# Delta-rule layer of a trunk kernel: what follows from a strip stands later in TensorE's order, the decays after the second keys, an own place for the substitution's tile

## Chip, cores and metric

The kernel runs on one core of a Trainium2 chip. The time is the device time of one execution in microseconds (us), shown as the median of several executions; lower is better. Inputs, weights and output are float32.

## What is computed

The reference is a trunk of four pre-norm residual layers over 256 tokens of width 1024: a pooling mixer, a gated delta-rule mixer, a latent attention, and a pooling mixer again. The change lies in the second, the delta-rule layer. Cut to what matters there:

```python
def gdn_mixer(h, w_in, conv_w, a_log, dt_bias, norm_g, w_out):
    proj = h @ w_in                               # 1024 -> 6160 columns
    qkv, gate, b_raw, a_raw = jnp.split(proj, ...)
    qkv = jax.nn.silu(causal_depthwise_conv(qkv, conv_w))
    q, k, v = jnp.split(qkv, [GDN_QK, 2 * GDN_QK], axis=-1)
    q = l2norm(...q) * (GDN_DK ** -0.5)           # 8 heads x 128
    k = l2norm(...k)                              # 8 heads x 128
    beta = sigmoid(b_raw); g = -exp(a_log) * softplus(a_raw + dt_bias)
    o = chunk_gated_delta_rule(q, k, v, g, beta)  # v: 8 heads x 256
    o = rmsnorm(o, norm_g) * silu(gate)
    return o @ w_out

def chunk_gated_delta_rule(q, k, v, g, beta):
    decay = jnp.exp(jnp.where(causal, diff, -jnp.inf))     # diff of summed g
    L = jnp.where(strict, (k_beta @ k.T) * decay, 0.0)
    sol = triangular_solve(I + L, [v_beta, k_beta * exp(g)])
    attn = jnp.where(causal, (q @ k.T) * decay, 0.0)
    ...
    # then from chunk to chunk: v_new = u - w @ state; o = q_dec @ state + attn @ v_new
```

## The kernel before

**Strips.** Every projection is cut into strips of 512 output columns over eight slices of the 1024 inputs. SyncE (SP) loads the weights in pieces of two slices, 512 KB each, into three buffers called `raw` (line 115). For float32 accuracy a slice is split in two parts: ScalarE (ACT) rounds it into `whi` (line 128), VectorE (DVE) or, for the slices named in `pool`, GpSimd (POOL) subtracts to get `wlo` (line 130). Each part has a ring of nine buffers, so that the splitting can be about a strip ahead of TensorE (PE). PE then does three products for every slice and column group. A strip that lands channel by channel (`chan=True`: keys, queries, values) is four units (pieces of weights) with 24 matmuls of 128x256 each, 96 in all; a strip of the gate is four units of 12 matmuls with 512 columns.

**The strips of the delta-rule layer**, in order: gate 0, keys 0, keys 1, queries 0, gate 1, values 0, queries 1, gate 2, values 1, values 2, values 3, gate 3, and then the output projection. After a strip of keys or queries (`channels`) ACT copies the four channel groups out of PSUM with the last tap of the convolution (`cv`, line 658), DVE adds three more taps to each (12 instructions, line 661), and ACT takes the Silu into the tile `kqT` (line 694). Values go the same way in two tiles `vc` (Silu in line 810).

**Side work.** What follows from a strip stands between the units of later strips; the lists handed to `keys`, `queries`, `gate` and `values` name it, one list for each gap after a unit (the first list after unit 0).
- `key_norms` and `query_norms` (through `squares`): PE transposes the four groups of `kqT` (8 transposes, `tp<-ident,kqT`, line 100), ACT squares them (line 705), DVE sums. `query_norms` has, on POOL, the product of `Eb` and the queries (`Gb<-Gb,kqT`, line 789) and a power for the norm.
- `lower` and `scored` (through `against`): 8 small matmuls (`aux<-kqT`), and 8 instructions on DVE that scale them by the decays `DT` into `LT` or the scores.
- `substitution`: eight DMAs write the diagonal blocks of `LT` to `d_l` in device memory (line 748), one reads them back as `Lb` (line 751), POOL does 31 pairs of instructions on `Lb`, `Tb` and `pr` (lines 756 and 760), and nine DMAs bring the result through `d_t` (line 762) into `T` (line 766). All these DMAs stand in SP's queue among the loads of weights.
- `values_turned`: 8 transposes of `vc` for two heads (`tp<-ident,vc`), and scaled copies into `vR` on ACT (line 823).
- `inverses` with `pairs`, `joined`, `turned`, `whole`, `last` (blocks of the inverse out of `T`), `news`, and the `step`s of the recurrence.
- `decays`: five Exp on ACT (line 651) over `DT` (two tiles), `Eb` (a name for the second `Gb` tile) and `eG`. Exp and Silu use different tables, and ACT loads a table when the function changes (ACT_TABLE_LOAD).

**What sets the order.** From `pinned["on"] = True` on, PE's instructions stand in the order of the program text. The other engines' order is made by a scheduler, which `later(...)` can hold back until a given instruction has been issued. Each engine works its queue strictly in order. Tiles called `big` share a pool of equal places; who gets the place of which earlier tile follows from the order of allocation, and a new owner waits for the last use by the old one. In this kernel `kqT_3639`, the output of queries 1, is given the place of `Lb`.

Of the kernel before, what the change touches and what calls it, by code (L numbers as in the profile page):

```python
# [12 lines left out]
AF = mybir.ActivationFunctionType  # L13
# [3 lines left out]
P = 128  # L17
D = 1024
S = 256
NT = S // P  # L20
# [22 lines left out]
def trunk(ctx: ExitStack, tc: tile.TileContext, x, positions, norm_g, pool_w_in, pool_w_grp,  # L43
# [3 lines left out]
    nc = tc.nc  # L47
# [22 lines left out]
    def big(name, *dims, dt=F32):  # L70
        return s4.tile([P, *dims], dt, tag="s4", name=name)
# [13 lines left out]
    def later(*instructions):  # L85

        order = ExitStack()
        for ins in instructions:
            order.enter_context(tc.issue_after(ins))
        return order  # L90


    pinned = {"on": False}
# [10 lines left out]
    mark = {}  # L104
# [333 lines left out]
    def pool_layer(i, j, hT):  # L438
# [64 lines left out]
        for g in order:  # L503
            gs = gate(g)
            if not place:
                with later(*[m for k, m in mark.items() if k != "rest"]):
                    turn_params()
                    window_counts()
            elif setups:
                with later(*[m for k, m in mark.items() if k != "rest"]):  # L510
                    setups.pop(0)()
            pT = pooled(g)
            if waiting:
                mixed(*waiting)
            waiting = (g, pT, gs)
# [46 lines left out]
    def gdn_layer(i, j, hT):  # L562
        H = GDN_H
        M = NT * H
# [13 lines left out]
        def gate(vi, *between):  # L578
            banks = project(cols_of(w_in, 2 * GDN_QK + GDN_V + vi * CW), units(KD), hT,
                            pool=() if vi else (0, 4), between=between)  # L580
            gs.append(big("gsg", NT, CW))
            for t in range(NT):
                gated = nc.scalar.activation(gs[vi][:, t, :], banks[t], AF.Silu)
            mark["gate"] = gated.ins
# [61 lines left out]
        Eb = Gb[1]  # L646

        def decays():
            with later(mark["gate"]):
                for a in (*DT, Eb, eG):  # L650
                    nc.scalar.activation(a, G if a is eG else a, AF.Exp)

# [11 lines left out]


        Q, B = 4, 32
        Tb = big("Tb", B, B)[:M * Q]
        nc.gpsimd.memset(Tb, 0.0)
        nc.gpsimd.memset(Tb.rearrange("m r c -> m (r c)")[:, ::B + 1], 1.0)
        T = [big("T", H, P) for _ in range(NT)]  # L670
# [13 lines left out]
        def channels(dst, c0, hf, which, between):  # L684

            banks = project(cols_of(w_in, c0 + hf * CW), units(KD), hT, chan=True,
                            pool=() if which else (0, 2, 4, 6), between=between)
            dst.append(big("kqT", 4, S))
            for b in range(2):
                cv = [worka("cv", S) for _ in range(2)]  # L690
                conv(*[(banks[b][:, c * S:(c + 1) * S], (c0 + hf * CW) // P + 2 * b + c, cv[c])
                       for c in range(2)])
                for c in range(2):
                    nc.scalar.activation(dst[hf][:, 2 * b + c, :], cv[c], AF.Silu)

        def squares(src, hf, which):

# [27 lines left out]
        def keys(hf, *between):  # L725
            channels(kT, GDN_QK, hf, 0, between)
# [11 lines left out]
        def lower(hf):  # L738
            for t in range(NT):
                against(LT, kT, s2, hf, t)  # L740

        def substitution():

            d_l = dram.tile([M * Q, B * B], F32, name="d_l")
            lv = d_l.rearrange("(t m d) (r c) -> t d r m c", t=NT, d=Q, r=B)
            for t in range(NT):
                for d in range(Q):
                    nc.sync.dma_start(out=lv[t, d],
                                      in_=LT[t][d * B:(d + 1) * B, :, d * B:(d + 1) * B])
            Lb = big("Lb", B, B)[:M * Q]  # L750
            nc.sync.dma_start(out=Lb, in_=d_l.rearrange("m (r c) -> m r c", r=B))
            pr = small("pr", 256, bufs=1)[:M * Q]
            for r in range(B - 1):
                n, c = B - 1 - r, r + 1
# [22 lines left out]
        def queries(hf, *between):  # L777
            channels(qT, 0, hf, 1, between)
# [52 lines left out]
        def inverses():  # L831
# [3 lines left out]


            U.extend(big("U", H, P) for _ in range(NT))
            X1 = [big("X1", H, P) for _ in range(NT)]
            for t in range(NT):
                nc.gpsimd.memset(X1[t][:, :, 32:64], 0.0)  # L840
                nc.vector.transpose(U[t].rearrange("p m c -> p (m c)"),
# [130 lines left out]
        def step(n):  # L972
            for m, stage in enumerate(stages):
                if 0 <= n - m < H:
                    stage(n - m)

        def do(f, *args):
            return lambda: f(*args)


        inv = lambda name, t: lambda: Us[name](t)
        keys(0)
        decays()
        pinned["on"] = True
        keys(1, (), (), [do(key_norms, 0)])
        queries(0, [do(lower, 0)], [do(key_norms, 1)], [do(lower, 1), substitution])
        gate(1, (), [do(query_norms, 0)], [do(scored, 0)])
        values(0)
        queries(1, (), (), [do(values_turned, 0)])
        gate(2, (), [do(query_norms, 1)], [do(scored, 1)])  # L990
        values(1)
        values(2, (), [do(values_turned, 1), inverses], [inv("pairs", 0)], [inv("pairs", 1)])
        values(3, [inv("joined", 0)], [inv("joined", 1), inv("turned", 0)],
               [do(values_turned, 2), inv("whole", 0), inv("turned", 1)],
               [inv("last", 0), inv("whole", 1)])
        gate(3, [inv("last", 1), do(news, 0)], [do(step, 0), do(values_turned, 3)],
             [do(news, 1), do(step, 1)], [do(step, 2)])
        for n in range(3, 6):
            step(n)
        return layer_out(gdn_w_out[j], yT, units(POOL_W // P), i,  # L1000
# [320 lines left out]
```

## Time and profile before

| what | value |
|---|---|
| time, median of 3 executions | 887.39 us (884.95 to 888.65) |
| the profiled execution's own time | 886.94 us |
| its span on the core | 885.2 us |
| mean granted TensorE clock | 0.975 |
| busy share of PE, DVE, ACT, POOL | 95%, 67%, 56%, 16% |
| PE's share of the chain that ended last | 83% |
| POOL's share of the same chain | 6% |
| weights and other data read from memory | 137.79 MB |

The page says how long each engine was busy in the span, then shows the span in 40 slices of 22.1 us with a digit for the busy tenths of each; a line PEclk gives the clock that TensorE was granted in each slice. Further views of the same execution list each instruction with its start, its duration and, in brackets, how long its engine stood idle before it and which instruction's end released it; and they sum such waits by line. The delta-rule layer's strips from keys 0 to the end of values 2 run from about 199 to 343 us of the span.

### The profile page before, as it was taken

Reading aid. Unit: us, or ns where it says so; the run is one execution under the profiler, and the core shown is the slowest. Engines: PE = TensorE matmul, PEld = TensorE weight load, DVE = VectorE, ACT = ScalarE, POOL = GpSimd, SP = SyncE. Lnnn points to the kernel's source line nnn. Section 1 sums busy time; section 2 is a strip of 40 time slices with the busy share of each in tenths; the row PEclk is TensorE's granted clock in tenths of the full one; section 3 lists DMA queues with packets and bytes.
Section 4 is the critical chain, followed back from the end, with each engine's and each line's share of the span. In section 5 each row is a group of like instructions: output and inputs, shape, how many; then the busy total and the mean of one; then the engine's idle time right before and its main releaser. Section 6 shows DMA issues by size and latency. Waiting matters only on the chain.

```text
span 885.2 us, 16118 instructions
## 1 busy us (share of the span) xinstructions
PE 844.9 (95%) x5967; PEld 784.7 (89%) x5967; DVE 594.7 (67%) x1144; ACT 494.6 (56%) x1009; POOL 144.1 (16%) x286
## 2 busy tenths in 40 slices
PE   7999999996899697999999999999999999999996
PEld 6999998986879597978898998999988989999986
DVE  5688776457777466646666666867877666867762
ACT  6655655467555353555556564556655565565542
POOL 4010001342249700012220201100000120000012
PEclk8999999998799799999999999999999999999999
DMA  6666556556346353222356766663444446665551
GB/s 236 200 190 202 180 176 214 156 175 184 96 119 183 88 170 105 93 78 96 123 148 195 221 169 162 187 190 97 129 143 134 146 129 204 201 202 183 191 200 49
DMA packets 111288, 140.43 MB, mean 159 GB/s; under 512 B 23340, under 2 KB 53224, under 8 KB 111208
## 3 DMA queue, kind: packets, MB, share of 16 engines
q1 hardware_dynamic: 109056, 138.17, 51.4%
q0 software_dynamic: 320, 1.06, 0.4%
q8 instruction: 47, 0.77, 0.4%
q10 hardware_dynamic: 1832, 0.16, 0.2%
q14 instruction: 33, 0.27, 0.1%
HBM read 137.79 MB, written 1.58 MB: 157 GB/s over the span
## 4 chain that ended last, share of the span: by engine, by line
PE 83%; POOL 6%; DVE 4%; DMA 2%; ACT 2%; issue 2%; SPq 0%; POOLq 0%; ACTq 0%; DVEq 0%
PE acc L96 68%; PE aux L96 12%; PE tp L100 3%; POOL Tb L760 2%; POOL pr L756 2%; DVE wlo L130 1%; DVE h L329 1%; DMA raw<-in_gdn_w_in_dram 1%; DMA gain<-in_norm_g_dram 1%; DMA Lb<-d_l 1%; DVE cv L661 1%; ACT junk L235 0%; ACT whi L128 0%; POOL xr L322 0%; DVE x L379 0%
## 5 line engine op out<-in xcount | busy, mean ns | idle before, releaser
L130 DVE TENSOR_TENSOR wlo<-raw,whi 128x512 fp32r<-128x512 f32 (+1 forms) x497 | 342.3, 710 | 190.2 <-ACT whi L128 181.7
L128 ACT CAST whi<-raw 128x512 fp32r<-128x512 f32 (+1 forms) x508 | 301.3, 617 | 269.9 <-PE acc L96 198.0
L96 PE MATMUL acc<-hTh,whi 128*128 128x256 f32 x832 | 237.5, 286 | 0.0
L96 PE MATMUL acc<-hTl,whi 128*128 128x256 f32 x832 | 236.8, 285 | 0.0
L96 PE MATMUL acc<-hTh,wlo 128*128 128x256 f32 x832 | 236.0, 284 | 0.0
L96 PEld LDWEIGHTS acc<-hTh,whi 128*128 128x128 f32 x832 | 159.5, 192 | 0.8
L96 PEld LDWEIGHTS acc<-hTl,whi 128*128 128x128 f32 x832 | 159.5, 192 | 0.4
L96 PEld LDWEIGHTS acc<-hTh,wlo 128*128 128x128 f32 x832 | 159.4, 192 | 0.1
L96 PE MATMUL acc<-whi,yTh 128*128 128x256 f32 (+1 forms) x384 | 116.8, 322 | 0.0
L96 PE MATMUL acc<-wlo,yTh 128*128 128x256 f32 (+1 forms) x384 | 116.4, 318 | 0.0
L96 PE MATMUL acc<-whi,yTl 128*128 128x256 f32 (+1 forms) x384 | 91.7, 318 | 0.0
L96 PEld LDWEIGHTS acc<-wlo,yTh 128*128 128x128 f32 x384 | 72.1, 188 | 5.0
L96 PEld LDWEIGHTS acc<-whi,yTh 128*128 128x128 f32 x384 | 71.9, 188 | 5.1
L96 PEld LDWEIGHTS acc<-whi,yTl 128*128 128x128 f32 x384 | 63.2, 188 | 5.9
L96 PE MATMUL acc<-whi,hTh 128*128 128x512 f32 (+1 forms) x144 | 58.6, 413 | 0.7 <-ACT hTh L221 0.7
L96 PE MATMUL acc<-wlo,hTh 128*128 128x512 f32 (+1 forms) x144 | 58.1, 407 | 0.5 <-DVE wlo L130 0.2
L317 POOL TENSOR_TENSOR hg<-x,gain 128x256 f32<-128x256 f32 x18 | 15.1, 843 | 260.3 <-DVE x L379 256.9
L96 PE MATMUL acc<-whi,hTl 128*128 128x512 f32 (+1 forms) x144 | 46.5, 397 | 0.0
L96 PEld LDWEIGHTS acc<-wlo,hTh 128*128 128x128 f32 x144 | 28.6, 199 | 7.1 <-DVE wlo L130 1.8
L96 PEld LDWEIGHTS acc<-whi,hTh 128*128 128x128 f32 x144 | 28.6, 199 | 7.0 <-ACT hTh L221 1.7
L96 PEld LDWEIGHTS acc<-whi,hTl 128*128 128x128 f32 x144 | 27.6, 195 | 5.9 <-DVE hTl L226 0.2
L461 POOL COPY win<-u 128x4 f32<-128x4 f32 x8 | 2.8, 353 | 177.4 <-ACT u L455 177.4
(330 smaller groups left out, 1420.2 us busy)
## 6 DMA issues: line engine op xcount, KB each, us to landing
raw<-in_pool_w_in_dram SPq DMA_DIRECT2D x60, 512.0 KB, 4.2
raw<-in_gdn_w_in_dram SPq DMA_DIRECT2D x48, 512.0 KB, 4.1
raw<-in_pool_w_out_dram SPq DMA_DIRECT2D x32, 512.0 KB, 3.7
raw<-in_mla_w_in_dram SPq DMA_DIRECT2D x24, 512.0 KB, 4.3
raw<-in_mla_w_uq_dram SPq DMA_DIRECT2D x36, 256.0 KB, 3.4
raw<-in_pool_w_grp_dram SPq DMA_DIRECT2D x16, 512.0 KB, 4.2
raw<-in_gdn_w_out_dram SPq DMA_DIRECT2D x16, 512.0 KB, 3.6
raw<-in_mla_w_ukv_dram SPq DMA_DIRECT2D x32, 256.0 KB, 3.0
```

The lines of the kernel that those rows point to most:

```text
L96: ins = nc.tensor.matmul(*args, **opts)
L100: ins = nc.tensor.transpose(*args)
L128: a = nc.scalar.copy(hi, v)
L130: b = e.tensor_tensor(out=lo, in0=v, in1=hi.bitcast(F32), op=ALU.subtract)
L317: nc.gpsimd.tensor_tensor(out=self.early[t, a], in0=xs[t][:, sl], in1=self.g[:, sl], op=ALU.mult)
L329: nc.vector.scalar_tensor_tensor(out=h[:, cut:], in0=xs[t][:, sl], scalar=r[:, 0:1], in1=self.g[:, sl], op0=ALU.mult, op1=ALU.mult)
L461: nc.gpsimd.tensor_copy(nxt[:, :, :d], cur[:, :, :d])
L661: nc.vector.scalar_tensor_tensor(out=o[:, d:], in0=ps[:, :S - d], scalar=tp(3 - d, c), in1=o[:, d:], op0=ALU.mult, op1=ALU.add)
L756: nc.gpsimd.tensor_tensor(out=pv, op=ALU.mult, in0=Lb[:, r, r + 1:, None].to_broadcast([M * Q, n, c]), in1=Tb[:, r:r + 1, :c].to_broadcast ...
L760: nc.gpsimd.tensor_tensor(out=tv, in0=tv, in1=pv, op=ALU.subtract)
```

## The change

The side work that follows from a strip of keys, queries or values stands later in PE's order, behind or near the end of the next strip: by one unit (norms of keys 0, turned values 0 and 1), two (norms of keys 1) or three units (norms of the queries). The norms of keys 0 come after the last unit of keys 1 (before: after its third unit, with `between` lists that begin with the first gap); those of keys 1, the second `lower` and the substitution after the last unit of queries 0; the norms of queries 0 and their scores in values 0; the turned values 0 after queries 1; the norms and scores of queries 1 in values 1; the turned values 1 and the inverses' first step in the third gap of values 2. The steps on the inverses follow in values 3 and gate 3, and `step(2)` and `news(1)` come after gate 3's last unit. A list that stands in the fourth place runs after the strip's last unit.

`decays` is called after keys 1 and held until the last Silu of keys 1 has been issued (`mark["kq"]`). The slices 0 and 4 of queries 0 get their subtraction on POOL. `Lb` and `Tb` keep names for their whole tiles, and the two tiles `X1` of the inverses use that memory after the substitution, so the pool gives `Lb` a place that no other tile takes.

```diff
-                with later(*[m for k, m in mark.items() if k != "rest"]):
+                with later(*[m for k, m in mark.items() if k not in ("rest", "kq")]):
...
         def decays():
-            with later(mark["gate"]):
+            with later(mark["gate"], mark["kq"]):
                 for a in (*DT, Eb, eG):
                     nc.scalar.activation(a, G if a is eG else a, AF.Exp)
...
-        Tb = big("Tb", B, B)[:M * Q]
+        Tb_ = big("Tb", B, B)
+        Tb = Tb_[:M * Q]
...
-                            pool=() if which else (0, 2, 4, 6), between=between)
+                            pool=(0, 4) if which and hf == 0 else () if which else (0, 2, 4, 6), between=between)
...
-                    nc.scalar.activation(dst[hf][:, 2 * b + c, :], cv[c], AF.Silu)
+                    mark["kq"] = nc.scalar.activation(dst[hf][:, 2 * b + c, :], cv[c],
+                                                      AF.Silu).ins
...
+        free = []
...
-            Lb = big("Lb", B, B)[:M * Q]
+            Lb_ = big("Lb", B, B)
+            Lb = Lb_[:M * Q]
+            free.extend((Lb_, Tb_))
...
-            X1 = [big("X1", H, P) for _ in range(NT)]
+            X1 = [a.rearrange("p (h a) c -> p h (a c)", h=H) for a in free]
...
         keys(0)
+        pinned["on"] = True
+        keys(1, (), (), (), [do(key_norms, 0)])
         decays()
-        pinned["on"] = True
-        keys(1, (), (), [do(key_norms, 0)])
-        queries(0, [do(lower, 0)], [do(key_norms, 1)], [do(lower, 1), substitution])
-        gate(1, (), [do(query_norms, 0)], [do(scored, 0)])
-        values(0)
-        queries(1, (), (), [do(values_turned, 0)])
-        gate(2, (), [do(query_norms, 1)], [do(scored, 1)])
-        values(1)
-        values(2, (), [do(values_turned, 1), inverses], [inv("pairs", 0)], [inv("pairs", 1)])
-        values(3, [inv("joined", 0)], [inv("joined", 1), inv("turned", 0)],
-               [do(values_turned, 2), inv("whole", 0), inv("turned", 1)],
-               [inv("last", 0), inv("whole", 1)])
-        gate(3, [inv("last", 1), do(news, 0)], [do(step, 0), do(values_turned, 3)],
-             [do(news, 1), do(step, 1)], [do(step, 2)])
+        queries(0, [do(lower, 0)], (), (), [do(key_norms, 1), do(lower, 1), substitution])
+        gate(1)
+        values(0, [do(query_norms, 0)], [do(scored, 0)])
+        queries(1, (), (), (), [do(values_turned, 0)])
+        gate(2)
+        values(1, [do(query_norms, 1)], [do(scored, 1)])
+        values(2, (), (), [do(values_turned, 1), inverses], [inv("pairs", 0)])
+        values(3, [inv("pairs", 1)], [inv("joined", 0)], [inv("joined", 1), inv("turned", 0)],
+               [inv("whole", 0), inv("turned", 1), do(values_turned, 2)])
+        gate(3, [inv("last", 0), inv("whole", 1)], [inv("last", 1), do(news, 0)], [do(step, 0)],
+             [do(step, 1), do(values_turned, 3)])
+        step(2)
+        news(1)
         for n in range(3, 6):
             step(n)
```

In the order of PE's instructions, the place where the norms of keys 0 (`kqT_2671`) are taken stands before ahead of the last unit of keys 1 (whose banks are `acc_2700` and `acc_2701`; the weights of its fourth unit begin with `whi_2829`):

```order
L96 MATMUL acc_2701<-hTh1_2267,whi_2777 128x256
L96 MATMUL acc_2701<-hTl1_2268,whi_2777 128x256
L96 MATMUL acc_2701<-hTh1_2267,wlo_2776 128x256
L100 MATMUL tp_2804<-ident_101,kqT_2671 128x128 x4
L100 MATMUL tp_2813<-ident_101,kqT_2671 128x128 x4
L96 MATMUL acc_2700<-hTh1_2267,whi_2829 128x256
L96 MATMUL acc_2700<-hTl1_2268,whi_2829 128x256
```

and now at the end of keys 1, ahead of the first matmuls of queries 0 (bank `acc_2885`):

```order
L96 MATMUL acc_2697<-hTh1_2267,whi_2807 128x256
L96 MATMUL acc_2697<-hTl1_2268,whi_2807 128x256
L96 MATMUL acc_2697<-hTh1_2267,wlo_2806 128x256
L100 MATMUL tp_2834<-ident_101,kqT_2671 128x128 x4
L100 MATMUL tp_2843<-ident_101,kqT_2671 128x128 x4
L96 MATMUL acc_2885<-hTh0_2258,whi_2890 128x256
L96 MATMUL acc_2885<-hTl0_2259,whi_2890 128x256
```

The two groups of transposes moved behind the last unit of keys 1, 24 matmuls. The number of PE's instructions is the same in both kernels.

In ACT's order, around the last Silus of keys 0 (`kqT_2671`) before:

```order
L694 ACT_TABLE_LOAD
L694 ACTIVATE kqT_2671<-cv_2672 128x256
L694 ACTIVATE kqT_2671<-cv_2673 128x256
L694 ACTIVATE kqT_2671<-cv_2684 128x256
L705 ACTIVATE sq_2809<-tp_2804 128x512
L651 ACT_TABLE_LOAD
L651 ACTIVATE DT_2496<-DT_2496 128x1024
L694 ACT_TABLE_LOAD
L694 ACTIVATE kqT_2671<-cv_2685 128x256
L705 ACTIVATE sq_2818<-tp_2813 128x512
L651 ACT_TABLE_LOAD
L651 ACTIVATE DT_2497<-DT_2497 128x1024
```

and now behind the last Silu of keys 1 (`kqT_2856`):

```order
L695 ACTIVATE kqT_2856<-cv_2858 128x256
L707 ACTIVATE sq_3046<-tp_3041 128x512
L695 ACTIVATE kqT_2856<-cv_2870 128x256
L651 ACT_TABLE_LOAD
L651 ACTIVATE DT_2496<-DT_2496 128x1024
L651 ACTIVATE DT_2497<-DT_2497 128x1024
L651 ACTIVATE Gb_2493<-Gb_2493 128x1024
L651 ACTIVATE eG_2484<-G_2483 128x16
L707 ACTIVATE sq_3055<-tp_3050 128x512
```

The Exps of `DT` left the Silus of keys 0 and stand in one block; the norms' second square (`sq_3055`) stands behind that block. Further down ACT's queue, ten casts `whi` (the last of them, `whi_3525`, out of `raw_3522`) now stand between the `cv` copies of queries 0 and its four Silus; before, two.

In SP's queue, where the substitution goes out and comes in (`raw` are weights; `d_l` and `Lb` the substitution's input), before:

```order
L115 DMA raw_3364<-in_gdn_w_in_dram 128x2x512
L748 DMA d_l_3047<-LT_2531 32x8x32 x4
L748 DMA d_l_3047<-LT_2532 32x8x32 x4
L115 DMA raw_3398<-in_gdn_w_in_dram 128x2x512
L751 DMA Lb_3056<-d_l_3047 64x1024
L115 DMA raw_3432<-in_gdn_w_in_dram 128x2x512
```

and now:

```order
L115 DMA raw_3488<-in_gdn_w_in_dram 128x2x512
L752 DMA d_l_3081<-LT_2531 32x8x32 x4
L115 DMA raw_3522<-in_gdn_w_in_dram 128x2x512
L752 DMA d_l_3081<-LT_2532 32x8x32 x2
L115 DMA raw_3556<-in_gdn_w_in_dram 128x2x512
L752 DMA d_l_3081<-LT_2532 32x8x32 x2
L115 DMA raw_3590<-in_gdn_w_in_dram 128x2x512
L757 DMA Lb_3090<-d_l_3081 64x1024
```

The eight writes of `d_l` stand three loads of weights later, with two loads among them: `raw_3522`, the second load of queries 1, now stands behind the first four writes, which need the whole first tile of `LT`. The result's way back stands now as follows, with three loads of values 3 (`raw_4189`, `raw_4233`, `raw_4287`) behind the write of `d_t` and among the reads of `T`:

```order
L115 DMA raw_4145<-in_gdn_w_in_dram 128x2x512
L768 DMA d_t_3155<-Tb_2514 64x1024
L115 DMA raw_4189<-in_gdn_w_in_dram 128x2x512
L772 DMA T_2517<-d_t_3155 32x8x32 x4
L772 DMA T_2518<-d_t_3155 32x8x32
L115 DMA raw_4233<-in_gdn_w_in_dram 128x2x512
L772 DMA T_2518<-d_t_3155 32x8x32 x3
L115 DMA raw_4287<-in_gdn_w_in_dram 128x2x512
```

Between the read of `Lb` and the write of `d_t` stand thirteen loads of weights, before twelve.

More of the change, by code (lines that the diff above doesn't have):

```diff
@@ L509, in pool_layer @@
             elif setups:
-                with later(*[m for k, m in mark.items() if k != "rest"]):
+                with later(*[m for k, m in mark.items() if k not in ("rest", "kq")]):
                     setups.pop(0)()
```

## The prediction

> **What bounds the kernel now.** First I read the page's share of TensorE (PE) and its clock in the 40 slices of 22.1 us:
>
> ```profile
> PE   7999999996899697999999999999999999999996
> PEclk8999999998799799999999999999999999999999
> ```
>
> PE is full nearly everywhere. Slices 10 to 16 (from 199 us on) are the exception, four of them with 6, 8, 6 and 7 tenths, and there the clock falls too. This is the delta-rule layer, the only place where the change moves much; at the start of the program it moves one transfer past another, which I cost at nothing. PE does the same instructions in both kernels. So the question is how much of PE's idle time goes, and how much of its slow time. Next the waits of PE in that stretch (195 to 345 us): total us, number of times, longest:
>
> ```profile
> PE tp L100 <- ACT kqT L694: 19.7, 9, 6.2
> PE tp L100 <- ACT vc L810: 6.7, 3, 3.6
> ```
>
> All 26.4 us are waits of a strip's own transposes for its Silu. One by one they are these rows of PE's timeline (start, duration, and in brackets the idle time before, with its releaser):
>
> ```profile
> 207.80 0.28 PE L96 MATMUL acc<-hTh,whi 128*128 128x256 f32 x1
> 209.81 0.28 PE L96 MATMUL acc<-hTh,wlo 128*128 128x256 f32 x1
> 213.05 1.30 PE L100 MATMUL tp<-ident,kqT 128*128 128x128 f32 x6 [2.96 <-ACT kqT L694]
> 218.68 0.69 PE L100 MATMUL tp<-ident,kqT 128*128 128x128 f32 x2 [4.33 <-ACT kqT L694]
> 252.66 0.66 PE L100 MATMUL tp<-ident,kqT 128*128 128x128 f32 x4 [1.09 <-ACT kqT L694]
> 254.36 0.46 PE L100 MATMUL tp<-ident,kqT 128*128 128x128 f32 x2 [1.04 <-ACT kqT L694]
> ```
>
> The first two rows are 17 matmuls apart, so one takes 0.118 us at full clock, a unit of 24 takes 2.8 us, a strip 11.3. Then keys 0 stop PE for 7.3 us, queries 0 for 2.1. Keys 1 stop it at 233.8 and 235.3; by the total of 19.7, keys 1 and queries 1 share the other 10.3. The waits for values are
>
> ```profile
> 332.83 0.66 PE L100 MATMUL tp<-ident,vc 128*128 128x128 f32 x4 [1.22 <-ACT vc L810]
> 337.07 1.12 PE L100 MATMUL tp<-ident,vc 128*128 128x128 f32 x4 [3.58 <-ACT vc L810]
> ```
>
> 4.8 us for values 1, which leaves 1.9 of the 6.7 for values 0. The long wait of queries 1 has another cause than its own strip. The view of the tile `Lb`, which shared its place with that output, says so:
>
> ```profile
> L756 POOL TENSOR_TENSOR pr<-Lb,Tb x31: 230/506/1056, 253.9 to 300.6; 64x31 f32<-64x31 f32 x2, 64x60 f32<-64x60 f32 x2, 64x87 f32<-64x87 f32 x2, 64x112 f32<-64x112 f32 x2
>   ACT kqT L694: 7.6, 1
> ```
>
> The first Silu of queries 1 waited 7.6 us for the last use of `Lb`, on GpSimd (POOL) up to 301 us, and PE behind it for 6.2 (the longest wait above).
>
> Second, the slow clock. The windows view, columns: us, busy us (and instructions) of PE, PEld, DVE, ACT, POOL, granted clock, DMA share, GB/s:
>
> ```profile
> 199.50:343.40 143.90, 117.44 (x793) 108.40 (x794) 96.56 (x208) 76.39 (x139) 58.56 (x87) 0.88 0.47 134
> 213.68:223.92 10.24, 5.91 (x29) 5.51 (x28) 7.67 (x24) 9.07 (x11) 1.95 (x2) 0.50 0.33 110
> 234.16:240.99 6.83, 6.15 (x30) 5.76 (x29) 3.68 (x11) 2.17 (x5) 2.84 (x3) 0.50 0.29 79
> 254.64:258.05 3.41, 3.41 (x11) 2.63 (x10) 0.69 (x1) 0.60 (x1) 2.86 (x9) 0.50 0.36 138
> 299.02:309.26 10.24, 6.38 (x18) 4.71 (x19) 3.06 (x5) 3.57 (x8) 5.11 (x11) 0.50 0.48 107
> 336.56:339.97 3.41, 2.90 (x14) 2.91 (x15) 0.00 (x0) 1.29 (x3) 0.00 (x0) 0.50 0.00 0
> ```
>
> Each stretch of half clock follows a wait of PE and lasts 3.41 us or a multiple. PE's busy time in the five, 5.91 + 6.15 + 3.41 + 6.38 + 2.90 = 24.75, would be half at full clock: 12.4 us lost. So the layer holds **26.4 + 12.4 = 38.8 us** that better order could return at most.
>
> **The change, part by part.** I followed each engine's new order with the durations of the old trace. The sum stands against the profiled execution's own 886.94 us (span 885.2 and 1.7 around it); the median of the runs is 887.39, which is 0.05% off, so one number serves both.
>
> *Norms of keys 0* move one unit, 2.8 us, later. What gated them is on ACT (first the start, then the duration):
>
> ```profile
> 211.28 1.28 ACT L694 ACT_TABLE_LOAD   x1
> 212.58 1.03 ACT L694 ACTIVATE kqT<-cv 128x256 f32<-128x256 f32 x3
> 214.50 1.28 ACT L651 ACT_TABLE_LOAD   x1
> 216.91 1.28 ACT L694 ACT_TABLE_LOAD   x1
> 218.21 0.42 ACT L694 ACTIVATE kqT<-cv 128x256 f32<-128x256 f32 x1
> ```
>
> The fourth Silu came 4.6 us behind the third, since an Exp and two table loads stood between. Without them four Silus end at about 214.0, and PE arrives at 209.9 + 2.8 = 212.8 and needs the second pair 0.5 us later. Left: about 0.5 us (between 0 and 1.2), no half clock. Before: 7.3 + 5.91/2 = 10.2. The Exps now stand behind the last Silu of keys 1, where the first `lower` needs `DT`, 24 matmuls (2.8 us) into queries 0; two table loads and three Exps are some 5 us, hidden for PE, since nothing of PE waits for `LT` until a PSUM bank is asked for again in gate 1.
>
> *Norms of keys 1* move two units, 5.7 us, later. But DVE gets there late. Its queue holds both decay tiles and the subtractions ahead of the twelve taps of keys 1:
>
> ```profile
> 213.61 2.19 DVE L643 SCALAR_TENSOR_TENSOR DT<-Gb,G,maskT 128x128 f32<-128x128 f32 x8 [1.90 <-DMA Gb<-d_g]
> 217.31 2.19 DVE L643 SCALAR_TENSOR_TENSOR DT<-Gb,G,maskT 128x128 f32<-128x128 f32 x8
> ```
>
> Before, PE stood for 7.3 us in that time and DVE caught up; now it doesn't get that pause. By my walk PE arrives at 226.7 and waits 2.3 us in two parts (bounds: 0, and twice that if two subtractions stand otherwise). Half clock follows for one stretch: 3.41/2 = 1.7. Left 4.0; before 2.5 + 6.15/2 = 5.6.
>
> *Norms of queries 0* move three units, and this is the part where I see a new wait. The casts for queries 1 now stand between the `cv` copies and the Silus of queries 0 on ACT. The last of them needs `raw_3522`, which stands on SP behind four writes of `d_l`; these wait for the second half of `LT`, which stands on DVE behind subtractions for values 0. In before the writes went at
>
> ```profile
> 243.59 3.79 SPq L748 DMA_DIRECT2D d_l<-LT  x8
> 301.14 0.46 SPq L762 DMA_DIRECT2D d_t<-Tb  x1
> 304.15 3.19 SPq L766 DMA_DIRECT2D T<-d_t  x6
> raw<-in_gdn_w_in_dram SPq DMA_DIRECT2D x48, 512.0 KB, 4.1
> ```
>
> and in the new order I get about 244.2 for the first, so four writes (1.9 us) and a load (4.1 us to landing) bring `raw_3522` at 250.2, the cast, a table load of 1.28 and the four Silus at 253.6. PE arrives at 246.2. **A wait of 6.4 us**, and half clock for one or two stretches (PE is busy in about 4.2 us of them): 2.1. Left 8.5; before 2.1 + 3.41/2 = 3.8. The bounds of the wait: nothing if the half of `LT` is done 6 us earlier, and 9 if the buffer comes free later too.
>
> *Turned values 0* move one unit: 2.8 us cover the 1.9. Left 0.
>
> *Norms of queries 1*: with an own place for `Lb` the Silus wait for DVE alone, and three units cover that. Before 7.8 + 6.38/2 = 11.0; left 0. What is late next is the substitution itself.
>
> *Turned values 1*: in before 4.8 + 2.90/2 = 6.3. The substitution starts later, I get 256.6 for 253.9, and POOL has more between its steps: the second queries' product and power fall into it as well as the first's:
>
> ```profile
> L789 POOL TENSOR_TENSOR Gb<-Gb,kqT 128x512 f32<-128x512 f32 x2 | 2.6, 1276 | 3.6 <-ACT kqT L694 3.6
> L682 POOL TENSOR_TENSOR rq<-rq,halves 128x8 f32<-128x8 f32 x2 | 3.3, 1650 | 0.1
> ```
>
> 47.2 us (253.9 to 301.1) and 2.9 more make 50, so it ends near 306.6. Then on SP: the write of `d_t`, 3.0 until the first read of `T` (301.14 to 304.15), eight reads at 0.53 and two loads among them at 0.4, so the last load, `raw_4287`, is issued near 315 and lands near 319. Its casts stand on ACT ahead of the Silu of values 1. So PE is through the turned values 1 near 321, with some 5.8 us of waits on the way, and 1.7 for a half clock. Left 7.5. Before, PE stood at this point of its work at 341.6.
>
> *The end of the layer*: `step(2)` and `news(1)` have no matmuls of gate 3 beside them now. I take 0, between 0 and 2.
>
> Sum: left 0.5 + 4.0 + 8.5 + 0 + 0 + 7.5 = 20.5 of 38.8, so **18.3 us** gone; the walk along the substitution gives 341.6 − 321 − 1.7 = 18.9. 886.94 − 18.9 = 868.0.
>
> [...] Two waits of 1.09 and 1.04 us, 1.7 us apart, were followed by 3.41 us at clock 0.50 (from 254.64). [...]
>
> **The rivals.**
>
> *All waits go* (chance 0.17). If `raw_3522` comes early (the `LT` half before 238) the substitution too starts some 6 us earlier; then 8.5 and most of 7.5 go as well, and 848 to 856 is left: 886.94 − 38.8 is the floor. For it: DVE is busy for only 96.56 of 143.90. Against it: the PE work of the layer without waits is 105 us, and then DVE would have to be busy 92% of the time.
>
> *Longer substitution or longer block* (0.13). POOL's same step takes
>
> ```profile
> 269.11 0.91 POOL L756 TENSOR_TENSOR pr<-Lb,Tb 64x231 f32<-64x231 f32 x1
> 287.87 0.58 POOL L756 TENSOR_TENSOR pr<-Lb,Tb 64x231 f32<-64x231 f32 x1
> ```
>
> 0.91 or 0.58. If the half of the 36 larger steps that are short become long too, 18 x 0.33 = 6 us come on top, one to one, as everything behind it is a chain: 874; with a longer block at queries 0, to 880. [...]
>
> *Slower* (0.05). The chain over POOL decides alone from the point where it ends after about 325 (306.6 + 18.9); each us behind that is a us lost, and one stretch of half clock adds 1.7. It could come so: POOL now has the product of queries 0 (`Gb<-Gb,kqT`) ahead of the substitution, which needs the Silu that waits for `raw_3522`. Were that Silu late by 25 us, the substitution ends near 332, and with another slow stretch the time is 868 + 25 + 1.7 = 895. For it: three queues wait for one another in turn. Against it: my walk has it 1.7 us before `Lb` lands.
>
> *Nothing to be measured* (0.05). The same chain, 15 to 22 us late, or `Lb`'s place used by another output after all. The new allocation gives the two different places, so I keep this small; the time is 883 to 890. Some 0.5%, 4.4 us, is about what the measurement can tell from no change.
>
> **How the numbers follow.** The forecast, 868, has 0.60: the terms' bounds give 859 to 875. The rivals have 0.17, 0.13, 0.05 and 0.05. The range goes from 853 (the better half of the first rival) to 879 (all but the end of the second). Faster by more than 4.4 us: 0.60 + 0.17 + 0.12; slower: 0.05; the rest, 0.06, within.
>
> **What would show it.** PE's waits for `kqT` should fall from 19.7 to about 9, nearly all at queries 0, just before 254; no Silu should wait for POOL. Table loads stand no more among the Silus of keys 0. POOL's last step should end at 305 to 308, and the last wait for `vc` near 320. If the wait at queries 0 is missing, I am wrong on the order of SP's queue; if POOL ends past 312, on the substitution; if the clock stays at 1.00 after waits of 2 us, on the slow stretches.

## The result, and the profile after

| kernel | median us | range, executions | ratio to before, 95% interval |
|---|---|---|---|
| before | 886.52 | 884.95 to 888.65, 4 | |
| changed | 872.02 | 870.94 to 875.96, 4 | 0.984 (0.980 to 0.988) |

The change makes the kernel 14.5 us faster, where 18.9 was forecast. The changed kernel's profiled execution is the slowest of its four, 875.96 us (span 874.3); a second profile of it, taken beside the later experiments, had 874.25 (span 872.5). Against the old profile's 886.94 the first one's gain is 11.0 us, so the rows below account for 11.0 and not for 14.5.

The page's slices after (22 us each) show the same seven slices of the delta-rule layer, 10 to 16, now with two at 7 tenths and one at 5:

```profile
PE   7999999999779959999999999999999999999996
PEclk8999999999889988999999999999999999999999
```

PE's waits after, by line (195 to 345 us; total, times, longest):

```profile
PE tp L100 <- ACT vc L816: 11.0, 2, 8.6
PE tp L100 <- ACT kqT L695: 10.0, 3, 5.4
```

The waits for `kqT` fell from 19.7 to 10.0, those for `vc` rose from 6.7 to 11.0. In PE's timeline they are five:

```profile
231.19 1.12 PE L100 MATMUL tp<-ident,kqT 128*128 128x128 f32 x4 [3.97 <-ACT kqT L695]
232.93 0.69 PE L100 MATMUL tp<-ident,kqT 128*128 128x128 f32 x2 [0.62 <-ACT kqT L695]
256.73 1.97 PE L100 MATMUL tp<-ident,kqT 128*128 128x128 f32 x8 [5.39 <-ACT kqT L695]
...
324.79 1.11 PE L100 MATMUL tp<-ident,vc 128*128 128x128 f32 x4 [8.57 <-ACT vc L816]
328.30 1.11 PE L100 MATMUL tp<-ident,vc 128*128 128x128 f32 x4 [2.39 <-ACT vc L816]
```

Norms of keys 0, turned values 0 and norms of queries 1 wait no longer. What is left stands at keys 1 (4.6), queries 0 (5.4) and the turned values 1 (11.0). The windows view has the slow clock at each of them (granted clock 0.50 in the last three rows; columns as in the prediction):

```profile
199.50:343.40 143.90, 122.95 (x888) 117.03 (x887) 108.27 (x224) 76.80 (x148) 63.91 (x89) 0.91 0.50 144
230.66:237.49 6.83, 5.67 (x24) 5.18 (x25) 3.92 (x12) 5.96 (x10) 0.00 (x0) 0.50 0.28 81
254.55:261.38 6.83, 4.65 (x22) 4.64 (x23) 1.97 (x3) 5.26 (x11) 1.29 (x2) 0.50 0.55 177
319.41:333.06 13.65, 5.87 (x27) 5.48 (x28) 8.05 (x13) 5.63 (x12) 0.00 (x0) 0.50 0.56 164
```

By the granted clock half of the busy time there, (5.67 + 4.65 + 5.87)/2 = 8.1 us, is lost beside the 21.0 of waits: 29.1 of the old 38.8. The view of the tile `Lb` shows the substitution (first and last start of its products):

```profile
L762 POOL TENSOR_TENSOR pr<-Lb,Tb x31: 232/608/1009, 261.4 to 313.2; 64x31 f32<-64x31 f32 x2, 64x60 f32<-64x60 f32 x2, 64x87 f32<-64x87 f32 x2, 64x112 f32<-64x112 f32 x2
```

It begins at 261.4 us, forecast 256.6, and ends 52.4 later at 313.8, forecast 306.6. The lines that lead to its start, on ACT and then on DVE:

```profile
230.20 0.62 ACT L128 CAST whi<-raw 128x512 fp32r<-128x512 f32 x1 [2.69 <-DMA raw<-in_gdn_w_in_dram]
230.72 0.41 ACT L695 ACTIVATE kqT<-cv 128x256 f32<-128x256 f32 x1
...
232.90 1.28 ACT L651 ACT_TABLE_LOAD   x1
234.19 2.00 ACT L651 ACTIVATE DT<-DT 128x1024 f32<-128x1024 f32 x2
...
254.32 0.62 ACT L128 CAST whi<-raw 128x512 fp32r<-128x512 f32 x1 [3.52 <-DMA raw<-in_gdn_w_in_dram]
256.25 1.34 ACT L695 ACTIVATE kqT<-cv 128x256 f32<-128x256 f32 x4
```

```profile
235.28 2.17 DVE L721 SCALAR_TENSOR_TENSOR LT<-aux,s,DT 128x128 f32<-128x128 f32 x8 [1.65 <-ACT DT L651]
...
247.19 2.15 DVE L721 SCALAR_TENSOR_TENSOR LT<-aux,s,DT 128x128 f32<-128x128 f32 x8
```

A cast that waits for its load stands ahead of the third Silu of keys 1; the Exps follow the fourth; DVE waits for them with the first half of `LT`; and the second half, which the substitution needs, comes at 247.2. A last cast that waits for its load stands ahead of queries 0's Silus. Then SP's queue:

```profile
248.32 1.82 SPq L752 DMA_DIRECT2D d_l<-LT  x4
...
253.25 0.40 SPq L115 DMA_DIRECT2D raw<-in_gdn_w_in_dram  x1
257.65 0.53 SPq L757 DMA_DIRECT2D Lb<-d_l  x1
...
313.81 0.46 SPq L768 DMA_DIRECT2D d_t<-Tb  x1
...
321.15 0.40 SPq L115 DMA_DIRECT2D raw<-in_gdn_w_in_dram  x1
```

The loads of values 3 stand behind `d_t`, which waits for POOL. PE's last wait for `vc` ends 14.5 us behind POOL's end (313.8 to 328.3); the walk had 14.4 (306.6 to 321). Before, it ended 36 us behind it (301.1 to 337.1): there PE's own work and its earlier waits set that time.

### The profile page after: what moved, and what is told of

Same layout as the page of the kernel before. It is cut to its first block, busy times and chain, and to the rows that moved or that the text cites. A ratio compares the mean times of both kernels' runs of the same rounds, so it can differ in the third digit from the quotient of the medians.

```text
span 874.3 us, 16119 instructions
## 1 busy us (share of the span) xinstructions
PE 839.3 (96%) x5967; PEld 782.2 (89%) x5967; DVE 597.6 (68%) x1142; ACT 490.3 (56%) x1006; POOL 150.2 (17%) x288
## 4 chain that ended last, share of the span: by engine, by line
PE 83%; POOL 7%; DMA 3%; DVE 3%; issue 1%; ACT 1%; SPq 0%; POOLq 0%; ACTq 0%; DVEq 0%
PE acc L96 68%; PE aux L96 12%; PE tp L100 3%; POOL Tb L766 3%; POOL pr L762 2%; DMA raw<-in_gdn_w_in_dram 2%; DMA gain<-in_norm_g_dram 1%; DVE h L329 1%; DVE wlo L130 1%; POOL xr L322 0%; ACT junk L235 0%; DMA Lb<-d_l 0%; POOL rq L683 0%; DVE x L379 0%; DVE cv L661 0%
```

## The experiments

**Question one: which part of the change brings the gain?** First the place of `Lb` alone, on the kernel before:

```diff
-        Tb = big("Tb", B, B)[:M * Q]
+        Tb_ = big("Tb", B, B)
+        Tb = Tb_[:M * Q]
...
-            Lb = big("Lb", B, B)[:M * Q]
+            Lb_ = big("Lb", B, B)
+            Lb = Lb_[:M * Q]
+            free.extend((Lb_, Tb_))
...
-            X1 = [big("X1", H, P) for _ in range(NT)]
+            X1 = [a.rearrange("p (h a) c -> p h (a c)", h=H) for a in free]
```

> The kernel before with one edit alone: Lb and Tb keep their whole tiles, X1 uses their memory, and so Lb's place is shared with no other output; the order of TensorE (PE) is that of before. Theory (two separate costs): the 7.8 us of waits of queries 1 and the slow clock behind them (6.4/2) go, and the substitution, which still ends near 301 us, frees values 1 near 301 + 14.5 = 316, when PE arrives there near 321; so nothing takes their place: 11 us less than before, 875 to 878 us. Rival (one chain): the wait comes back at the turned values 1, behind the loads that stand after the write of d_t; then the gain is at most 4 us, 883 us or more, and the waits for vc rise from 6.7 to over 12.

Measured: 880.93 us, ratio 0.994 (0.993 to 0.996), between the two. PE's waits in its trace:

```profile
PE tp L100 <- ACT kqT L695: 15.6, 8, 4.5
PE tp L100 <- ACT vc L815: 9.0, 3, 3.6
```

The Silu no longer waits for POOL: queries 1 stop PE for 2.8 us instead of 7.8, now for DVE, and with small changes elsewhere 4.1 us of waits for `kqT` go. The waits for `vc` grow by 2.3. The last of them, 3.58 us, is the same as before; what grew is the first one of values 1, from 1.22 to 3.42, up to 326.6. ACT ahead of it:

```profile
319.74 0.62 ACT L128 CAST whi<-raw 128x512 fp32r<-128x512 f32 x1 [1.35 <-DMA raw<-in_gdn_w_in_dram]
320.27 0.84 ACT L658 ACTIVATE vc<-acc,tap 128x256 f32<-128x256 f32 x2
...
325.89 0.63 ACT L815 ACTIVATE vc<-vc 128x512 f32<-128x512 f32 x1 [1.39 <-DVE vc L661]
```

PE is there 8 us earlier than before, and the Silu (the last row) comes too late for it. The cast is one of five on ACT between 305 and 320 us that end a pause until a load, and it stands between the copies of values 1 out of PSUM. The loads go out behind the write of `d_t` at 300.1. So my theory was half right: some 5 of the 11 us are won. What comes back has the rival's cause, the loads behind `d_t`, at a much smaller size than it said (waits for `vc` of 9.0 us, not over 12).

Then the order without the place:

```diff
-            X1 = [a.rearrange("p (h a) c -> p h (a c)", h=H) for a in free]
+            X1 = [big("X1", H, P) for _ in range(NT)]
```

(and `Lb`, `Tb` as before the change).

> The changed kernel without the edit on Lb, Tb and X1 (X1 gets tiles of its own again). In the new order the pool gives Lb and the output of queries 1 different places even so. Theory: the edit on the places does nothing in this order, 870 to 875 us, as the changed kernel. Rival (the place is what counts): X1 now takes the place of the output of queries 1 and U that of Lb, and a wait for them, at the inverses, costs over 3 us: 876 us or more.

Measured: 873.13 us, ratio 0.986 (0.984 to 0.988); the changed kernel had 0.984 (0.980 to 0.988). In the new order the place brings nothing that can be measured: the pool gives different places anyway, and in this trace too no Silu waits for `Lb`. So the gain comes with the new order, together with the two edits that follow.

The decays back ahead of keys 1:

```diff
-        keys(1, (), (), (), [do(key_norms, 0)])
         decays()
+        keys(1, (), (), (), [do(key_norms, 0)])
...
-            with later(mark["gate"], mark["kq"]):
+            with later(mark["gate"]):
```

> The changed kernel with decays() called ahead of keys 1 and held only until gate 0's Silus, as before the change. The Exps and table loads stand among the Silus of keys 0 again: a wait of 4 to 6 us at the norms of keys 0. Theory (the waits ahead of the substitution's start add to it): the start moves 2 to 5 us later than in the changed kernel, 874 to 878 us. Rival (VectorE and the loads catch up in that wait, and keys 1 then wait less): the start moves by less than 1 us, 871 to 873 us.

Measured: 868.31 us, ratio 0.980 (0.978 to 0.982): faster than the changed kernel, which neither side expected. The changed kernel itself, run again beside other experiments:

> The changed kernel as it is, once more, beside the three others. Both theories: 870 to 874 us. If decays_back (868.3) is really faster, this one stays above 870.5.

It gave 873.20, ratio 0.985 (0.983 to 0.987). The two intervals don't meet: **this part of the change costs some 4 to 5 us** (4.9 by these medians, 4.1 by the ratios, each to its own series of the kernel before; 3.7 against the changed kernel's first series, whose wider interval does meet that of decays_back). The wait of 4 to 6 us at the norms of keys 0 that I had expected isn't there. ACT in decays_back:

```profile
211.01 1.34 ACT L695 ACTIVATE kqT<-cv 128x256 f32<-128x256 f32 x4
...
212.88 1.28 ACT L651 ACT_TABLE_LOAD   x1
...
218.55 1.10 ACT L651 ACTIVATE DT<-DT 128x1024 f32<-128x1024 f32 x1
```

With the norms of keys 0 later, the four Silus of keys 0 stand together even so, and the Exps fall into a time in which PE waits for nothing. Its DVE has the second half of `LT` here:

```profile
240.10 2.15 DVE L721 SCALAR_TENSOR_TENSOR LT<-aux,s,DT 128x128 f32<-128x128 f32 x8
```

7.1 us earlier than in the changed kernel; the substitution starts at 253.6 instead of 261.4, no table load stands before the Silus of queries 0, and PE's wait there is 0.3 us.

The two subtractions of queries 0 back on DVE:

```diff
-                            pool=(0, 4) if which and hf == 0 else () if which else (0, 2, 4, 6), between=between)
+                            pool=() if which else (0, 2, 4, 6), between=between)
```

> The changed kernel with the subtractions of slices 0 and 4 of queries 0 back on VectorE (DVE). Theory (DVE is late at keys 1): 2 x 0.69 us more on DVE there, the wait at keys 1 grows by about 1.4 us, and with it the start of the substitution; 873 to 875 us. Rival (the Silus of keys 1 wait for a load whose buffer POOL's slower subtraction frees late): same or up to 2 us faster, 870 to 872.

Measured: 878.82 us, ratio 0.991 (0.989 to 0.992), 5.6 us slower than the changed kernel beside it. The direction was the theory's, the size not. Two casts now stand ahead of the fourth Silu of keys 0, one of them with a wait for its load:

```profile
216.69 0.62 ACT L128 CAST whi<-raw 128x512 fp32r<-128x512 f32 x1 [2.45 <-DMA raw<-in_gdn_w_in_dram]
...
217.71 0.41 ACT L695 ACTIVATE kqT<-cv 128x256 f32<-128x256 f32 x1
```

and PE waits 3.8 us there, where the changed kernel doesn't; the substitution starts at 263.3 for the 259.9 of the changed kernel beside it. So two small edits that don't touch PE's order are worth some 4 to 6 us each. Of these two parts of the change the decays' new place costs time and the subtractions on POOL save it, and in both traces the order on ACT ahead of the substitution differs from the changed kernel's.

**Question two: what makes the wait at queries 0, and is it worth its 5.4 us?** The transfers to the substitution on POOL's queue:

```diff
-                    nc.sync.dma_start(out=lv[t, d],
+                    nc.gpsimd.dma_start(out=lv[t, d],
...
-            nc.sync.dma_start(out=Lb, in_=d_l.rearrange("m (r c) -> m r c", r=B))
+            nc.gpsimd.dma_start(out=Lb, in_=d_l.rearrange("m (r c) -> m r c", r=B))
```

> The changed kernel with the eight writes of d_l and the read of Lb issued by GpSimd (POOL) instead of SyncE (SP). Theory (SP's queue): raw_3522 no longer stands behind them, so the wait of 5.4 us at queries 0 falls below 1.5 us; the end of the layer follows the substitution one to one: it starts 3 to 4 us earlier than 261.4, and the time is 866 to 870 us. Rival (VectorE is late anyway): the Silus of queries 0 wait for the casts as before, the wait stays over 4 us and the time within 2 us of the changed kernel's 872.

Measured: 874.77 us, ratio 0.987 (0.985 to 0.989); the wait at queries 0 is 6.75 us, and the substitution starts at 260.9. The theory fails. The rival holds for the wait; its bound on the time is missed by 0.8 us (874.77 against 872 plus 2). DVE and SP there:

```profile
244.85 2.14 DVE L721 SCALAR_TENSOR_TENSOR LT<-aux,s,DT 128x128 f32<-128x128 f32 x8
246.92 1.28 DVE L130 TENSOR_TENSOR wlo<-raw,whi 128x512 fp32r<-128x512 f32 x2
```

```profile
247.63 1.96 SPq L115 DMA_DIRECT2D raw<-in_gdn_w_in_dram  x2
```

The load goes out at 247.63, when the first of the two subtractions behind `LT` has ended (near 247.6) and its buffer is free; the writes of `d_l` aren't what it waits for. The wait is made by the casts ahead of the Silus, whatever delays their load. Holding those casts back:

```diff
+        after = held_back["after"]
+        held_back["after"] = [*after, mark["kq"]]
         queries(1, (), (), (), [do(values_turned, 0)])
+        held_back["after"] = after
```

> The changed kernel with the splitting of queries 1's weights held back until the last Silu of queries 0 has been issued, so that on ScalarE (ACT) no cast of queries 1 stands ahead of the Silus of queries 0. The wait of PE at queries 0 (5.4 us) should fall below 1.5 us. Theory (one chain over the substitution decides): PE only arrives sooner at the turned values 1 and waits there longer; the waits for vc rise from 11 to about 16, and the time falls by 0 to 3 us, to 869 to 872. Rival (the waits add up): 5.4 us and the slow clock behind it (6.83/2) go, 863 to 865.

Measured: 873.41 us, ratio 0.986 (0.984 to 0.987). The wait at queries 0 is gone, and the time is the changed kernel's (872.02 and 873.20), a little above the theory's 869 to 872:

```profile
PE tp L100 <- ACT vc L816: 18.2, 3, 15.4
PE tp L100 <- ACT kqT L695: 2.8, 2, 1.9
```

The waits for `kqT` fall by 7.2 us and those for `vc` rise by 7.2: all of it comes back at the turned values 1, as the theory of one chain has it.

**Question three: does the substitution decide?** The start of its first step on POOL, the span of the profiled execution, and their difference, for all kernels that have it whole, the new order, and `d_t` on SP:

| kernel | start | span | span less start |
|---|---|---|---|
| decays_back | 253.6 | 865.8 | 612.2 |
| order_only | 258.8 | 871.8 | 613.0 |
| silus_first | 259.3 | 872.1 | 612.8 |
| changed, again | 259.9 | 872.5 | 612.6 |
| in_pool | 260.9 | 874.1 | 613.2 |
| changed | 261.4 | 874.3 | 612.9 |
| dve_split | 263.3 | 877.2 | 613.9 |

Over 9.7 us of start the span follows nearly one to one, within 0.9 us of 613; PE's waits ahead of it play no part beyond the start that they cause (silus_first has 7.2 us less of them). The start itself differs by 1.5 us between the two profiles of the changed kernel. Before, the difference was 885.2 − 253.9 = 631.3, and 627.0 in own_place. So what stands behind the substitution's start takes 18 us less in the new order, and the start is 7.5 us later.

Leaving out steps of the substitution:

```diff
-            for r in range(B - 1):
+            for r in range(B - 10):
```

> The changed kernel with the last 9 of the 31 steps of the substitution left out (its result is then incomplete), some 10 us of POOL. Theory (one chain): POOL ends near 302 to 304 instead of 313.8, the waits for vc fall from 11.0 to below 3 us and the slow stretch behind them from 13.65 to 6.83 us or less; 859 to 863 us. Rival (the end of values 1 is bound by VectorE or by the loads anyway): waits for vc stay over 6 us, 866 us or more.

Measured: 866.97 us, ratio 0.980 (0.977 to 0.982). Both numbers of the rival hold, by little: the waits for `vc` are 6.2 us. POOL ends at 299.7, 14 us earlier, and the time falls by 5 to 6. (The trace is of the slowest execution, 871.88; the other four took 866.7 to 867.3.) The edit did more than it says: with fewer steps the scheduler put `d_t` ahead of four more loads, nine instead of thirteen behind `Lb`. The first load behind `d_t` goes out at 300.34, and this is the cast on ACT that comes next:

```profile
304.91 0.62 ACT L128 CAST whi<-raw 128x512 fp32r<-128x512 f32 x1 [9.15 <-PE acc L96]
```

The load goes out when POOL has ended, and the cast that needs it ends a pause of ACT of 9.15 us (the row names PE as its releaser, but it fits the load: 4.3 us is the median from issue to landing of these loads in the changed kernel). PE's last wait for `vc` ends at 323.7, now 24 us behind POOL's end. As a test of the substitution's length this run is inconclusive; it shows that loads of weights waited for POOL at both places of `d_t`: the first behind it went out at 300.34 here and at 314.36 in the changed kernel, 0.6 us behind POOL's end both times.

So the way back on POOL's queue:

```diff
-            nc.sync.dma_start(out=d_t.rearrange("m (r c) -> m r c", r=B), in_=Tb)
+            nc.gpsimd.dma_start(out=d_t.rearrange("m (r c) -> m r c", r=B), in_=Tb)
...
-                    nc.sync.dma_start(out=T[t][d * B:(d + 1) * B, :, d * B:(d + 1) * B],
+                    nc.gpsimd.dma_start(out=T[t][d * B:(d + 1) * B, :, d * B:(d + 1) * B],
```

> The changed kernel with the write of d_t and the reads of T issued by POOL instead of SP. Theory (SP's queue): the loads of values 3 no longer wait for the end of the substitution, so the 11.0 us of waits for vc at values 1 fall below 4 us; T itself lands near 322 to 325 us, so pairs wait for it for some 2 to 5 us: 860 to 865 us. Rival (the substitution decides whatever the queue): the wait moves whole to the pairs, and the time stays over 868 us.

Measured: 865.11 us, ratio 0.975 (0.972 to 0.978). PE's waits:

```profile
PE aux L96 <- DMA T<-d_t: 3.7, 1, 3.7
PE tp L100 <- ACT vc L816: 1.4, 1, 1.4
```

As the theory says: the waits for `vc` fall from 11.0 to 1.4, and what is late next is `T` itself, by 3.7 us; the time is 0.1 us above its 860 to 865. Not all of the gain is the queue's. In this trace the substitution starts at 257.1, although ACT's order at keys 0 and keys 1 is that of the changed kernel: the load that holds a Silu of keys 1 went out earlier (SP's five loads of that stretch begin at 216.23 for 218.50), and keys 1 stop PE for 1.9 us instead of 4.6. The span less the start is 865.7 − 257.1 = 608.6 for 613, so some 4 us come from the queue; what made the load go out earlier is open. With queries 1's casts held back as well:

> The same edit on the kernel out_pool (write of d_t and reads of T issued by POOL, 865.1 us). Theory (one chain): 862 to 865 us, and the wait of PE for the read of T grows from 3.7 to about 8 us. Rival (the waits add up): 857 to 859.

Measured: 866.21 us, ratio 0.976 (0.974 to 0.979): again no gain from a shorter wait at queries 0, and above the theory's 862 to 865; PE's wait for `T` grew to 5.4 us, less than the 8 of the theory.

**A version that beats both.** decays_back with the way back on POOL's queue:

> decays_back (decays called ahead of keys 1) with the write of d_t and the reads of T issued by POOL. Theory (the two are steps of one chain and both shorten it: an earlier start of the substitution, and no loads behind its end): POOL ends near 305, the first matmuls of the pairs wait for T until about 315, 857 to 862 us. Rival (out_pool had taken all that PE can gain here): 864 us or more.

Measured: 862.04 us, ratio 0.971 (0.969 to 0.973), as the theory has it; POOL ends at 308.6, though, not near 305. PE still waits 2.6 us for `T`. And with the query norms' scalings and powers behind the substitution on POOL:

```diff
-                nc.gpsimd.tensor_tensor(out=tv, in0=tv, in1=pv, op=ALU.subtract)
+                mark["sub"] = nc.gpsimd.tensor_tensor(out=tv, in0=tv, in1=pv,
+                                                      op=ALU.subtract).ins
...
+            with later(mark["sub"]):
                 nc.gpsimd.tensor_scalar(qh, ssq[:, 1, :, 4 * hf:4 * hf + 4], float(P), EPS * P,
                                         ALU.mult, ALU.add)
                 power(rh, qh)
```

(the two lines behind `power` stand under `later` too).

> back_out with the scalings and powers of both query norms (POOL) held until the last step of the substitution; they are used only in the recurrence. Theory (every us of POOL in the substitution counts while PE waits for T): POOL ends 4 to 5 us earlier than in back_out, PE's wait for T falls below 1.5 us, and the time is 3 to 6 us less, 853 to 858. Rival (POOL is no longer the last to arrive): within 1.5 us of back_out.

Measured: **857.18 us, ratio 0.967 (0.965 to 0.970)**, 29 us less than before and 16 less than the changed kernel beside it. Its wait for `T`:

```profile
PE aux L96 <- DMA T<-d_t: 1.1, 1, 1.1
```

POOL ends 3.7 us earlier than in back_out, and 4.9 us are won by the medians; single executions of the two overlap (857.9 to 863.9, and 854.7 to 861.4), so that size is rough. In the four kernels with the way back on POOL's queue the span less the start is 604.5 to 608.6. Most of what is left stands at keys 1, with 5.1 and 0.6 us of waits.

## Why the prediction was right, and where its sizes were off

- **What bounds the kernel, and what the order returns:** right. The waits at keys 0, values 0 and queries 1 went as forecast (0.5, 0 and 0 us left; measured none), and new ones came at queries 0 and values 1, where the walk put them. The sign that the waits for `kqT` would stand nearly all at queries 0 did not come: 4.6 of the 10.0 stand at keys 1.
- **Norms of keys 1**, 4.0 us forecast: 4.6 + 5.67/2 = 7.4 in the first profile; the second has waits of 4.3 and 0.8. DVE was named as the cause, and it is one of two: its last taps, below, end at 229.0 and 230.0, PE is there at 227.2, so DVE alone makes some 2.2 us, near the 2.3 forecast. The other 1.7 are the cast that waits 2.69 us for its load, ahead of the third Silu on ACT.

```profile
228.50 0.48 DVE L661 SCALAR_TENSOR_TENSOR cv<-acc,tap,cv 128x253 f32<-128x253 f32 x1
...
229.49 0.48 DVE L661 SCALAR_TENSOR_TENSOR cv<-acc,tap,cv 128x253 f32<-128x253 f32 x1
```

- **Norms of queries 0**, 8.5 forecast: 5.4 + 4.65/2 = 7.7. The size was right, the cause only in part. "`raw_3522` stands behind four writes of `d_l`" is true of the queue, but without those writes the wait stays (in_pool). What makes it is that casts stand ahead of the Silus (silus_first); their last load waits for a buffer that DVE frees behind the second half of `LT` (in_pool).
- **Turned values 1**, 7.5 forecast: 11.0 + 5.87/2 = 13.9. This is the mis-sized term, and by the prediction's own sign (POOL past 312) it was wrong on the substitution. It took the substitution to start at 256.6 and to last 50 us; it started at 261.4 and lasted 52.4. Of the 4.8 us at the start, 4.1 stand ahead of the first write of `d_l` (248.32 for 244.2), and that waits for the late second half of `LT`. Its 62 steps took 41.9 us on POOL for 38.9 before, by the rows below (two groups of 31 steps each, first before, then after). These 3 us have the direction of the second rival, which put 6 on it. DVE was busy for 108.3 of 143.9 us, before for 96.6; whether that or something else lengthened the steps, no run shows.

```profile
L760 POOL TENSOR_TENSOR Tb<-Tb,pr 64x31 f32<-64x31 f32 (+15 forms) x31 | 20.2, 652 | 2.4
L756 POOL TENSOR_TENSOR pr<-Lb,Tb 64x31 f32<-64x31 f32 (+15 forms) x31 | 18.7, 604 | 14.1 <-DMA Lb<-d_l 12.0
```

```profile
L766 POOL TENSOR_TENSOR Tb<-Tb,pr 64x31 f32<-64x31 f32 (+15 forms) x31 | 22.5, 727 | 2.2
L762 POOL TENSOR_TENSOR pr<-Lb,Tb 64x31 f32<-64x31 f32 (+15 forms) x31 | 19.4, 627 | 4.5 <-DMA Lb<-d_l 2.4
```

- **The sum:** 20.5 us left were forecast, 29.1 measured, so 9.7 of the 38.8 are gone: 886.94 − 9.7 = 877.2 against the profiled 875.96. The walk along the substitution comes a little nearer: POOL ended 7.2 us later than forecast (313.8 for 306.6), and 868.0 + 7.2 = 875.2. The median, 872.0, lies below both because the profiled execution was the slowest of the four; no trace shows what the others did faster.
- **An edit costed at nothing:** "two table loads and three Exps are some 5 us, hidden for PE, since nothing of PE waits for `LT` ...". PE doesn't, but the substitution does, and through it the end of the layer: decays_back starts it at 253.6 and is 4 to 5 us faster. This is the step whose reasoning was wrong: the cover was looked for on PE alone.
- **An edit not costed:** the two subtractions on POOL are worth 5.6 us here. The two omissions are of opposite sign and nearly the same size. That they leave the forecast near the result is luck.
- **Adding up waits:** the terms don't add. With the wait at queries 0 removed the time stayed (873.41). The forecast's second walk, along the substitution, was the right one.
- **Slow clock behind short waits:** not every such wait was followed by it. In back_out_norms a wait of 1.12 us for `T` was followed by 3.41 us at 0.50, and one of 1.45 us by none:

```profile
311.55 0.66 PE L100 MATMUL tp<-ident,vc 128*128 128x128 f32 x4 [1.45 <-ACT vc L818]
316.17 1.97 PE L96 MATMUL aux<-T,LT 128*128 128x64 f32 x16 [1.12 <-DMA T<-d_t]
```

```profile
311.55:318.20 6.65, 5.53 (x46) 5.36 (x47) 1.83 (x2) 3.55 (x8) 4.30 (x10) 1.00 0.41 116
318.20:321.61 3.41, 3.41 (x18) 3.41 (x18) 3.41 (x7) 0.62 (x1) 0.00 (x0) 0.50 0.16 17
```

So the length of a wait alone does not decide it; what does stays open.

## What to carry to other kernels

When PE's order is moved to hide waits, look for the one slow chain on a side engine (here the substitution on POOL), date its start and its end, and price every edit by what it does to those two. Here waits of PE ahead of the start cost nothing by themselves, while work that "nothing of PE waits for" cost 4 to 5 us. Transfers that waited for a side engine held up the loads behind them in the queue (in the changed kernel SP issued none from 302.1 us until the write of `d_t` at 313.8): taking the way back out of it brought some 4 us, taking the way in out brought none. A cast made for later weights that stood ahead of queries 0's Silus made them wait for the cast's load (ACT stood 3.52 us until it landed) and for that load's buffer (in_pool); the 5.4 us that this cost PE became free only because the substitution decided.

## What the hardware showed unexpectedly

Small transfers were late where large ones stood among them. The view of the tile `d_l` gives the time from issue to landing of the eight writes of 32 KB, before

```profile
DMA to landing us min/median/max: 1.6/1.7/1.7
```

and in the changed kernel, where two loads of 512 KB stand among them:

```profile
DMA to landing us min/median/max: 1.6/1.7/5.2
```

The slowest took 5.2 us for 1.7, and `Lb` is read only when all have landed: SP issued that at 257.65, though its last write of `d_l` went out before 253.25. From the first write to the first step on POOL it is 13.0 us (248.3 to 261.4) for the 10.3 of before (243.6 to 253.9). On POOL's queue (in_pool), with SP's loads beside them, the same writes took 1.9 to 6.0 us. In both traces loads of 512 KB went out while the writes did; whether they made the writes late, and by what means, no run shows.
